# Finer release of attention work in a 512-column mixer, with the first softmax scaling moved into the norm

## The chip, the cores and the metric

The kernel runs on 1 core of a Trainium2 chip. The metric is the device time of one launch in microseconds (us). Before the change it is 2238.53 us, the median of 3 runs (2237.58 to 2239.18).

## The reference

Two layers act on 256 latent tokens and 256 context tokens of 1024 channels. Each layer is a half-weight SwiGLU feed-forward, a mixer, and a second feed-forward, each between RMS norms with modulation. The mixer makes one combined input projection of the normed tokens and runs two branches on it: retention with 4 heads, and differential attention with 8 heads, which the change touches. Context tokens read context tokens only, latent tokens read all 512; the last layer needs the latent output alone.

```python
def diff_attend(q, k, v, lam):
    s = jnp.einsum('bhiqd,bhikd->bhiqk', q, k).astype(jnp.float32) * (DIFF_DH ** -0.5)
    p = jax.nn.softmax(s, axis=-1)
    a = p[:, :, 0] - lam * p[:, :, 1]
    return jnp.einsum('bhqk,bhke->bhqe', a.astype(v.dtype), v)

def diff_output(o, subln_w, lam_init):
    o = rmsnorm(jnp.transpose(o, (0, 2, 1, 3)), subln_w) * (1.0 - lam_init)
    return o.reshape(o.shape[0], o.shape[1], -1)
```

The norm is taken over the 128 channels of one head and one token. EPS is 1e-6.

## The kernel before

Every product in fp32 is three matmuls on TensorE (`mm3`, L340 to L342): the operands are split into a high part and a remainder, and high by high, high by low and low by high are summed in PSUM. Weights are split as they arrive: ScalarE casts (L164), VectorE subtracts (L165). A projection block of the mixer is either `tok` (128 tokens by 512 columns, 24 matmuls) or `projT` (two times 128 channels, 48 matmuls of 512 columns when both token kinds are wanted, of 256 when only latent tokens are). These blocks run one behind the other and are meant to keep TensorE fed. The results of a Q or K block of the attention are turned by the rotary tables on VectorE and split by casts on ScalarE (L567, L571, L572) and subtractions on VectorE (L569).

The attention itself is side work. A generator `diff_attn` handles one pair of heads: `score` issues 4 matmuls into PSUM (L651, L652), takes a row maximum (L653), the exponentials of both maps on ScalarE with their row sums (L659), scales the first map by its reciprocal sum (L665) and adds the second, times minus lambda and its own reciprocal (L666). Three scores later `weigh` transposes the result (L678), copies it out of PSUM (L680) and multiplies it by V (L684). At the fourth `weigh` of a token kind comes the norm tail: square (L689), sum (L691), `rstd_of` on GpSimd (L264 and the power L266), and four scaled writes (L697). In layer 0 a pair of heads has 11 steps (latent and context queries), in layer 1 it has 7. There are four pairs, d0 to d3 below, and four retention heads, r0 to r3, driven in the same way.

`defer` puts a generator into the queue `sideq` with a due time, counted in ticks; `tick` advances the clock at places among the projections and takes steps from the first generator in the queue. `need` runs the queue until a named generator is finished. A tile scheduler then orders the instructions of each engine by what they depend on, so the order on an engine is near the program's but not equal to it. PSUM has 8 banks: a score of latent queries holds 2, a score of context queries 1, a K block 2, the others 1.

```python
n = -(-sideq[0][2] // max(1, sideq[0][1] - clock[0]))
while n > 0 and sideq:
    step()
    n -= 1
```

Of the kernel before, what the change touches and what calls it, by code (L numbers as in the profile page):

```python
# [14 lines left out]
AF = mybir.ActivationFunctionType  # L15
# [5 lines left out]
KD = 8  # L21
# [13 lines left out]
def build(ctx, tc, a):  # L35
# [74 lines left out]
    def slot(shape, dt=F32):  # L110
        return slots.get(shape, dt)
# [7 lines left out]
    def small(n, tag):  # L119
        return sm.tile([P, n], F32, tag=tag, name=tag)  # L120
# [141 lines left out]
    def rstd_of(ss, n, w=1):  # L262
        m = small(8, "rm")
        pool.tensor_scalar(out=m[:, :w], in0=ss, scalar1=1.0 / n, scalar2=EPS, op0=ALU.mult, op1=ALU.add)  # L264
        r = small(8, "rr")
        pool.tensor_tensor(out=r[:, :w], in0=m[:, :w], in1=cneg[:, :w], op=ALU.pow)  # L266
        return r
# [184 lines left out]
    def mixer(l, st, AB, fetch, after):  # L452
# [10 lines left out]
        sideq = deque()  # L463
        done = set()
        pend = []
        clock = [0]

        def step():
            it = sideq[0]
# [7 lines left out]
        def tick():  # L477
            clock[0] += 1
            if sideq:
                n = -(-sideq[0][2] // max(1, sideq[0][1] - clock[0]))  # L480
                while n > 0 and sideq:
                    step()
                    n -= 1

        def defer(key, gen, within, steps):
            sideq.append([gen, clock[0] + within, steps + 1, key])
# [5 lines left out]
        def flush():  # L492
            while pend:
                pend.pop(0)()

        def tok(ws, t, ev):
            bk = bank()
            for k in range(KD):
                wt = ws[k // 2].rearrange("p s (k n) -> p s k n", k=2)
                mm3(bk, h[k // 2][:, k % 2, 0, t * P:(t + 1) * P], h[k // 2][:, k % 2, 1, t * P:(t + 1) * P],  # L500
                    wt[:, 0, k % 2], wt[:, 1, k % 2], k == 0, k == KD - 1)
            flush()
            post = ev(t, bk)
            banks.put(bk)
            if post is not None:
                pend.append(post)
            tick()
# [10 lines left out]
        def projT(b, pairs, ev):  # L518
            ws = [split(r) for r in load(a["winT"][l, b])]
            n = 256 * len(pairs)  # L520
            if len(pairs) == 2:
                b0 = banks.two()
                bk = b0
            else:
                b0 = bank()
                bk = b0.rearrange("p (j n) -> p j n", j=2)
            for j in range(2):
                js = slice(j * P, (j + 1) * P)
                for k in range(KD):
                    wt = ws[k // 4].rearrange("p s (k n) -> p s k n", k=4)  # L530
                    mm3(bk[:, j], wt[:, 0, k % 4, js], wt[:, 1, k % 4, js], h[k // 2][:, k % 2, 0, 0:n],
                        h[k // 2][:, k % 2, 1, 0:n], k == 0, k == KD - 1)
                if j == 0:
                    flush()
                    if len(pairs) == 2:
                        tick()
            for c in pairs:
                ev(c, bk[:, :, c * 256:(c + 1) * 256])
            banks.put(b0)
            tick()  # L540
# [96 lines left out]
        def diff_attn(u, KH, KL, Q, dv):  # L637
            lag = deque()
            ch = (u % 2) * 256

            def score(c, k0, NK, t, hh):
                if c == LAT:
                    b0 = banks.two()
                    sb = b0
                else:
                    b0 = bank()
                    sb = b0.rearrange("p (m n) -> p m n", m=2)
                mx = small(2, "mx")
                for m in range(2):
                    qs = Q[m][:, hh, t * P:(t + 1) * P]  # L650
                    mm(sb[:, m], lhsT=qs, rhs=KH[m][:, hh, k0:k0 + NK], start=True, stop=False)  # L651
                    mm(sb[:, m], lhsT=qs, rhs=KL[m][:, hh, k0:k0 + NK], start=False, stop=True)  # L652
                dve.reduce_max(mx, sb, axis=AX.X)  # L653
                nb = small(2, "nb")
                dve.tensor_scalar(out=nb, in0=mx, scalar1=-0.125, scalar2=None, op0=ALU.mult)
                e = tmp4([P, 2, 512])
                se = small(2, "se")
                for m in range(2):
                    act(e[:, m, :NK], sb[:, m], AF.Exp, bias=nb[:, m:m + 1], scale=0.125, accum_out=se[:, m:m + 1])  # L659
                banks.put(b0)  # L660
                rc = small(2, "rc")
                dve.reciprocal(rc, se)
                r1 = small(1, "r1")
                dve.tensor_tensor(out=r1, in0=rc[:, 1:2], in1=K["nlam"], op=ALU.mult)
                dve.tensor_scalar(out=e[:, 0, :NK], in0=e[:, 0, :NK], scalar1=rc[:, 0:1], scalar2=None, op0=ALU.mult)  # L665
                dve.scalar_tensor_tensor(out=e[:, 0, :NK], in0=e[:, 1, :NK], scalar=r1, in1=e[:, 0, :NK],  # L666
                                         op0=ALU.mult, op1=ALU.add)
                return e[:, 0]

            obs = {}  # L670

            def weigh(c, k0, NK, tt, hh, e):
                if tt == 0 and hh == 0:
                    obs[c] = bank()
                ob = obs[c].rearrange("p (t n) -> p t n", t=2)
                tb = bank()
                for i in range(NK // P):
                    nc.tensor.transpose(tb[:, i * P:(i + 1) * P], e[:, i * P:(i + 1) * P], ident)  # L678
                aT = tmp2()
                nc.scalar.copy(aT[:, :NK], tb[:, :NK])  # L680
                banks.put(tb)
                for i in range(NK // P):
                    kt = k0 // P + i
                    mm(ob[:, tt, hh * P:(hh + 1) * P], lhsT=aT[:, i * P:(i + 1) * P],  # L684
                       rhs=dv[kt // 2][:, kt % 2, ch + hh * P:ch + (hh + 1) * P], start=i == 0, stop=i == NK // P - 1)
                if tt == 0 or hh == 0:
                    return
                sq = tmp2([P, 2, 256])
                act(sq, ob, AF.Square)  # L689
                ss = small(4, "oss")  # L690
                dve.reduce_sum(ss, sq.rearrange("p t (h d) -> p (t h) d", h=2), axis=AX.X)  # L691
                r = rstd_of(ss, P, 4)
                if (u // 2, c) not in o:
                    o[u // 2, c] = slot([P, 2, 512])
                for tt in range(2):
                    for hh in range(2):
                        dve.scalar_tensor_tensor(out=o[u // 2, c][:, tt, ch + hh * P:ch + (hh + 1) * P],  # L697
                                                 in0=ob[:, tt, hh * P:(hh + 1) * P],
                                                 scalar=r[:, 2 * tt + hh:2 * tt + hh + 1], in1=K["sub"],
                                                 op0=ALU.mult, op1=ALU.mult)  # L700
                banks.put(obs[c])

            for c in QP:
                k0, NK = (0, 512) if c == LAT else (256, 256)
                for tt in range(2):
                    for hh in range(2):
                        if len(lag) == LAG:
                            weigh(*lag.popleft())
                        lag.append((c, k0, NK, tt, hh, score(c, k0, NK, 2 * c + tt, hh)))
                        yield  # L710
            while lag:
                weigh(*lag.popleft())
                yield
            slots.put(*KH, *KL, *Q)
            if u % 2:
                slots.put(*dv)
# [140 lines left out]

        rkq = {}

        def rkq_blocks(z):  # L860
            kk = [slot([P, 2, 512], F32R) for _ in range(2)]
            projT(2 + z, BOTH, ev_ret(kk[0], kk[1], 128 ** -0.5))
            qq = [slot([P, 2, 512], F32R) for _ in range(2)]
            projT(z, QP, ev_ret(qq[0], qq[1], 1.0))
            rkq[z] = (kk, qq)
# [9 lines left out]
        def pick(both, lat):  # L875
            return lat if last else both
# [7 lines left out]
            tok(ws, t, ev_V(dv))  # L884
        K.update(mixer_consts())
        kq = diff_blocks(0)
        diff_defer(0, kq, dv, pick(5, 4))
        kq = diff_blocks(1)
        diff_defer(1, kq, dv, pick(6, 5))
        need("d0")  # L890
        rkq_blocks(0)
        rv_block(0, pick(4, 2), pick(8, 5))
        need("d1")
        wide(8, QP, ev_gB(0))
        kq = diff_blocks(2)
# [1 line left out]
        dv = [slot([P, 2, 512]) for _ in range(2)]  # L897
        wide(5, BOTH, ev_V(dv))
        flush()
        diff_defer(2, kq, dv, pick(6, 4))  # L900
        wide(2, QP, ev_rg(0, False))
        kq = diff_blocks(3, "d2")
        diff_defer(3, kq, dv, pick(7, 5))
        wide(6, QP, ev_gA(0))
        rkq_blocks(1)
        need("d3")
        rv_block(1, pick(4, 2), pick(7, 4))
        wide(9, QP, ev_gB(1))
        wide(3, QP, ev_rg(1, True))
        need("r3")  # L910
# [175 lines left out]
```

## Time and profile before

| | |
|---|---|
| median of 3 runs | 2238.53 us |
| the profiled execution, its own time | 2237.81 us |
| its span, first to last instruction | 2236.0 us |
| TensorE busy, share of the span | 96% |
| VectorE, ScalarE, GpSimd busy | 62%, 39%, 6% |
| mean granted TensorE clock, of full speed | 0.986 |

The profile comes from one execution on the chip. "Busy" counts an instruction from its start to its modelled end; in the timeline and in the groups by line the text behind "<-" names the engine, tile and line that ended the idle time before an instruction. In rows of matmuls the issue distance is read from the starts, since one begins while the one before it still drains. A granted clock of 1.0 is TensorE's upper level, 2.4 GHz, and 0.5 is 1.2 GHz.

### The profile page before, as it was taken

Reading aid. Unit: us, or ns where it says so; the run is one execution under the profiler, and the core shown is the slowest. Engines: PE = TensorE matmul, PEld = TensorE weight load, DVE = VectorE, ACT = ScalarE, POOL = GpSimd, SP = SyncE. Lnnn points to the kernel's source line nnn. Section 1 sums busy time; section 2 is a strip of 40 time slices with the busy share of each in tenths; the row PEclk is TensorE's granted clock in tenths of the full one; section 3 lists DMA queues with packets and bytes.
Section 4 is the critical chain, followed back from the end, with each engine's and each line's share of the span. In section 5 each row is a group of like instructions: output and inputs, shape, how many; then the busy total and the mean of one; then the engine's idle time right before and its main releaser. Section 6 shows DMA issues by size and latency. Waiting matters only on the chain. (4 is left out here: it accounts for less than half of the span.)

```text
span 2236.0 us, 27616 instructions
## 1 busy us (share of the span) xinstructions
PE 2150.1 (96%) x10694; PEld 1799.5 (80%) x10694; DVE 1377.9 (62%) x2180; ACT 866.1 (39%) x1367; POOL 131.6 (6%) x248
## 2 busy tenths in 40 slices
PE   7999999989999999999999999999998999898998
PEld 4888888767877888888888788888876788787997
DVE  3798372677667764596243389635257676677454
ACT  3322232564345433532232242223245455455443
POOL 1000000200100010200000110000020010001000
PEclk8999999999999999999999999999999999999999
DMA  9766342211222234465334256724322133355554
GB/s 336 247 224 225 101 135 94 88 47 61 91 69 76 81 102 151 130 206 174 102 110 146 85 174 214 252 95 142 101 71 95 61 112 114 117 179 184 183 187 132
DMA packets 85059, 306.98 MB, mean 137 GB/s; under 512 B 9968, under 2 KB 10048, under 8 KB 84928
## 3 DMA queue, kind: packets, MB, share of 16 engines
q1 hardware_dynamic: 81648, 295.73, 39.9%
q0 software_dynamic: 2848, 8.43, 1.4%
q8 instruction: 83, 1.36, 0.2%
q10 hardware_dynamic: 432, 1.06, 0.1%
q14 instruction: 48, 0.39, 0.1%
HBM read 304.10 MB, written 1.09 MB: 136 GB/s over the span
## 5 line engine op out<-in xcount | busy, mean ns | idle before, releaser
L165 DVE TENSOR_TENSOR w<-raw,w 128x1024 fp32r<-128x1024 f32 x408 | 497.6, 1222 | 442.5 <-ACT w L164 438.6
L164 ACT CAST w<-raw 128x1024 fp32r<-128x1024 f32 x408 | 427.8, 1053 | 645.6 <-PE ps L342 585.4
L340 PE MATMUL ps<-h,w 128*128 128x512 f32 (+1 forms) x1856 | 664.5, 360 | 8.4 <-ACT t L659 7.4
L341 PE MATMUL ps<-h,w 128*128 128x512 f32 (+1 forms) x1856 | 664.2, 358 | 0.0
L342 PE MATMUL ps<-h,w 128*128 128x512 f32 (+1 forms) x1856 | 662.3, 358 | 0.4 <-DVE w L165 0.4
L340 PEld LDWEIGHTS ps<-h,w 128*128 128x128 f32 x1856 | 352.4, 191 | 63.3 <-ACT t L659 8.3
L341 PEld LDWEIGHTS ps<-h,w 128*128 128x128 f32 x1856 | 353.1, 190 | 50.1 <-issue 0.8
L342 PEld LDWEIGHTS ps<-h,w 128*128 128x128 f32 x1856 | 352.2, 190 | 50.3 <-DVE w L165 0.8
L184 DVE CUSTOM_DVE_ANT_0 jd<-r,r 128x1024 bf16<-128x1024 f32 x224 | 273.3, 1220 | 6.4 <-DMA r<-wada_dram 1.6
L340 PE MATMUL ps<-w,h 128*128 128x512 f32 x544 | 212.6, 392 | 3.7 <-ACT t L659 3.1
L341 PE MATMUL ps<-w,h 128*128 128x512 f32 x544 | 212.8, 392 | 0.6 <-DVE w L165 0.6
L342 PE MATMUL ps<-w,h 128*128 128x512 f32 x544 | 212.3, 391 | 0.0
L340 PE MATMUL ps<-w,gs 128*128 128x512 f32 x504 | 196.2, 389 | 0.0
L341 PE MATMUL ps<-w,gs 128*128 128x512 f32 x504 | 196.1, 389 | 0.0
L342 PE MATMUL ps<-w,gs 128*128 128x512 f32 x504 | 196.1, 389 | 0.0
L369 ACT ACTIVATE t<-ps 128x512 f32<-128x512 f32 (+1 forms) x88 | 47.9, 544 | 252.7 <-PE ps L342 252.7
L340 PEld LDWEIGHTS ps<-w,h 128*128 128x128 f32 x544 | 102.2, 188 | 25.1 <-ACT t L659 4.0
L370 DVE TENSOR_TENSOR r<-ps,t 128x512 f32<-128x512 f32 (+1 forms) x88 | 54.7, 622 | 109.4 <-PE ps L342 80.4
L341 PEld LDWEIGHTS ps<-w,h 128*128 128x128 f32 x544 | 102.2, 188 | 21.7 <-DVE w L165 2.2
L342 PEld LDWEIGHTS ps<-w,h 128*128 128x128 f32 x544 | 102.2, 188 | 20.6
L340 PEld LDWEIGHTS ps<-w,gs 128*128 128x128 f32 x504 | 94.6, 188 | 19.8
L342 PEld LDWEIGHTS ps<-w,gs 128*128 128x128 f32 x504 | 94.6, 188 | 19.7
(175 smaller groups left out, 2167.5 us busy)
## 6 DMA issues: line engine op xcount, KB each, us to landing
raw<-fin_dram SPq DMA_DIRECT2D x176, 512.0 KB, 4.2
r<-wada_dram SPq DMA_DIRECT2D x144, 512.0 KB, 5.1
raw<-fout_dram SPq DMA_DIRECT2D x88, 512.0 KB, 3.6
raw<-winW_dram SPq DMA_DIRECT2D x80, 512.0 KB, 3.6
raw<-winT_dram SPq DMA_DIRECT2D x48, 512.0 KB, 4.0
raw<-wout_dram SPq DMA_DIRECT2D x16, 512.0 KB, 5.1
r<-scr POOLq DMA_DIRECT2D x10, 512.0 KB, 5.2
r<-cc_dram SPq DMA_DIRECT2D x7, 512.0 KB, 5.7
```

Of the source, the lines that this page charges most:

```text
L164: keep(nc.scalar.copy(w[:, 0, :], src))
L165: keep(dve.tensor_tensor(out=w[:, 1, :], in0=src, in1=w[:, 0, :], op=ALU.subtract))
L184: dve.tensor_tensor_reduce(out=junk, in0=r[j], in1=cs[c], scale=1.0, scalar=0.0, op0=ALU.mult, op1=ALU.add, accum_out=out[:, c, 2 * u + j: ...
L340: mm(o, lhsT=wH, rhs=xH, start=start, stop=False)
L341: mm(o, lhsT=wH, rhs=xL, start=False, stop=False)
L342: mm(o, lhsT=wL, rhs=xH, start=False, stop=stop)
L369: act(sg[:, :N], ab[0][:, :N], AF.Silu)
L370: dve.tensor_tensor(out=g[f // 2][:, f % 2, :N], in0=ab[1][:, :N], in1=sg[:, :N], op=ALU.mult)
```

## The change

1. The tick now adds steps left over ticks left to a credit and takes a step for each whole unit of it; before, the quotient was rounded up, so at least one step was taken at every tick. Ticks come every 12 matmuls of 512 columns: two in a `tok` block (before: one), four in a `projT` block of both token kinds (before: two), and two in one of latent tokens alone (before: one). The due times are longer in ticks, mostly about twice.
2. d0 has to be finished between the K and the Q block of the first retention projections instead of before them.
3. The first map is no longer divided by its row sum. Its exponentials are used as they are, the second map gets minus lambda times the first sum over the second, and the missing factor is put into the norm: the sum of squares is multiplied by the squared reciprocal of the first sum ahead of the root, and the root's result by the reciprocal. The VectorE operation L665 (48 times) goes away; for each norm tail (12 times) one small VectorE reciprocal and three small GpSimd products come in, two of which stand between the sum and the norm's writes.

```diff
         def tick():
             clock[0] += 1
             if sideq:
-                n = -(-sideq[0][2] // max(1, sideq[0][1] - clock[0]))
-                while n > 0 and sideq:
+                credit[0] += sideq[0][2] / max(1, sideq[0][1] - clock[0])
+                while credit[0] >= 1 and sideq:
                     step()
-                    n -= 1
+                    credit[0] -= 1
+            else:
+                credit[0] = 0
...
                     wt[:, 0, k % 2], wt[:, 1, k % 2], k == 0, k == KD - 1)
+                if k == 3:
+                    tick()
             flush()
...
-                if j == 0:
-                    flush()
-                    if len(pairs) == 2:
+                    if k == 7 and j == 0:
+                        flush()
+                    if j * KD + k in ((3, 7, 11) if len(pairs) == 2 else (7,)):
                         tick()
...
+                if c not in sall:
+                    sall[c] = small(8, "sall").rearrange("p (m i) -> p m i", m=2)
+                i4 = 2 * (t % 2) + hh
...
                 for m in range(2):
-                    act(e[:, m, :NK], sb[:, m], AF.Exp, bias=nb[:, m:m + 1], scale=0.125, accum_out=se[:, m:m + 1])
+                    act(e[:, m, :NK], sb[:, m], AF.Exp, bias=nb[:, m:m + 1], scale=0.125,
+                        accum_out=sall[c][:, m, i4:i4 + 1])
                 banks.put(b0)
-                rc = small(2, "rc")
-                dve.reciprocal(rc, se)
+                rc = small(1, "rc")
+                dve.reciprocal(rc, sall[c][:, 1, i4:i4 + 1])
                 r1 = small(1, "r1")
-                dve.tensor_tensor(out=r1, in0=rc[:, 1:2], in1=K["nlam"], op=ALU.mult)
-                dve.tensor_scalar(out=e[:, 0, :NK], in0=e[:, 0, :NK], scalar1=rc[:, 0:1], scalar2=None, op0=ALU.mult)
+                dve.scalar_tensor_tensor(out=r1, in0=rc, scalar=K["nlam"], in1=sall[c][:, 0, i4:i4 + 1],
+                                         op0=ALU.mult, op1=ALU.mult)
...
                 dve.reduce_sum(ss, sq.rearrange("p t (h d) -> p (t h) d", h=2), axis=AX.X)
+                n0 = small(4, "n0")
+                dve.reciprocal(n0, sall[c][:, 0, :])
+                n2 = small(4, "n2")
+                pool.tensor_tensor(out=n2, in0=n0, in1=n0, op=ALU.mult)
+                pool.tensor_tensor(out=ss, in0=ss, in1=n2, op=ALU.mult)
                 r = rstd_of(ss, P, 4)
+                pool.tensor_tensor(out=r[:, :4], in0=r[:, :4], in1=n0, op=ALU.mult)
...
-        def rkq_blocks(z):
+        def rkq_blocks(z, before=None):
             kk = [slot([P, 2, 512], F32R) for _ in range(2)]
             projT(2 + z, BOTH, ev_ret(kk[0], kk[1], 128 ** -0.5))
+            if before:
+                need(before)
...
-        diff_defer(0, kq, dv, pick(5, 4))
+        diff_defer(0, kq, dv, pick(12, 10))
         kq = diff_blocks(1)
-        diff_defer(1, kq, dv, pick(6, 5))
-        need("d0")
-        rkq_blocks(0)
-        rv_block(0, pick(4, 2), pick(8, 5))
+        diff_defer(1, kq, dv, pick(16, 14))
+        rkq_blocks(0, "d0")
+        rv_block(0, pick(8, 4), pick(16, 10))
...
-        diff_defer(2, kq, dv, pick(6, 4))
+        diff_defer(2, kq, dv, pick(12, 8))
...
-        diff_defer(3, kq, dv, pick(7, 5))
+        diff_defer(3, kq, dv, pick(16, 10))
...
-            rv_block(1, pick(4, 2), pick(7, 4))
+            rv_block(1, pick(8, 4), pick(16, 8))
```

The first number of a pair is for layer 0, the second for layer 1.

How the order of the instructions moves is shown at three places. In these rows an operand named `h` is the mixer's input, `w` a split weight, and what follows "waits" is the engine on whose progress the instruction waits.

The first place is TensorE in layer 1, from the third score of d0 on (the first two stand ahead of these rows in both orders). Before:

```order
L651 MATMUL ps<-r_12378,r_12464 128x512 [waits Activation_49]
L652 MATMUL ps<-r_12380,r_12464 128x512
L651 MATMUL ps<-r_12379,r_12465 128x512 [waits Activation_49]
L652 MATMUL ps<-r_12381,r_12465 128x512
L678 MATMUL ps<-ident,t_12582 128x128 [waits DVE_49]
L678 MATMUL ps<-ident,t_12582 128x128 x3
L651 MATMUL ps<-r_12378,r_12464 128x512 [waits Activation_49]
L652 MATMUL ps<-r_12380,r_12464 128x512
L684 MATMUL ps<-r_12148,t_12614 128x128 [waits Activation_49]
```

And of the change (the scores are L658 and L659 there, the transposes L685, the product with V L691):

```order
L658 MATMUL ps<-r_12370,r_12456 128x512 [waits Activation_49]
L659 MATMUL ps<-r_12372,r_12456 128x512
L658 MATMUL ps<-r_12371,r_12457 128x512 [waits Activation_49]
L659 MATMUL ps<-r_12373,r_12457 128x512
L340 MATMUL ps<-h,w 128x256 [waits Activation_49]
L341 MATMUL ps<-h,w 128x256
L342 MATMUL ps<-h,w 128x256
L340 MATMUL ps<-h,w 128x256
```

Before, the transposes of the first score and the fourth score follow the third score at once, and the 48 projection matmuls of 256 columns of d1's Q block stand in one piece behind d0's third product with V. Now 19 of these 48 stand between the third score and the first transposes, 6 between those and the product with V, and 23 behind the second transposes, ahead of the fourth score.

The second place is ScalarE in the same stretch. Before, the row of L659 for the third score's second map, the copies and the casts of d1's K block up to the fourth score's exponentials:

```order
L659 ACTIVATE t_12628,se<-ps,nb 128x512
L680 COPY t_12690<-ps 128x512 [waits PE_49]
L680 COPY t_12718<-ps 128x512 [waits PE_49,Activation_49]
L567 CAST r_12536<-ps 64x2x256 [waits DVE_49]
L567 CAST r_12536<-t_12662 64x2x256 [waits DVE_49]
L571 CAST r_12536<-t_12662 64x2x256
L567 CAST r_12537<-t_12662 64x2x256
...
L567 CAST r_12537<-ps 64x2x256
L659 ACTIVATE t_12704,se<-ps,nb 128x512 [waits Activation_49]
```

Of the change (the casts are L571, L575 and L576, the exponentials L665, the copies L687):

```order
L665 ACTIVATE t_12603,sall<-ps,nb 128x512
L571 CAST r_12528<-ps 64x2x256 [waits DVE_49]
L687 COPY t_12651<-ps 128x512 [waits PE_49,Activation_49]
L571 CAST r_12528<-t_12623 64x2x256 [waits DVE_49]
...
L571 CAST r_12529<-ps 64x2x256
L665 ACTIVATE t_12665,sall<-ps,nb 128x512 [waits DVE_49]
L575 CAST r_12529<-ps 64x2x256 [waits DVE_49]
...
L687 COPY t_12713<-ps 128x512 [waits PE_49]
...
L665 ACTIVATE t_12727,sall<-ps,nb 128x512 [waits DVE_49,PE_49,Activation_49]
```

Before, the exponentials of three scores stand ahead of the casts and the fourth behind them; now those of two stand ahead and the third behind. Ten casts lie between in both.

The third place is GpSimd at two norm tails of layer 0. Before:

```order
L264 TENSOR_SCALAR rm<-oss 128x4 [waits DVE_49]
L266 TENSOR_TENSOR rr<-rm,cneg 128x4 [waits Pool_49]
L264 TENSOR_SCALAR rm<-oss 128x4 [waits DVE_49]
L266 TENSOR_TENSOR rr<-rm,cneg 128x4 [waits Pool_49]
L784 TENSOR_SCALAR gm<-bmv 128x1 [waits DVE_49]
L785 TENSOR_TENSOR gr<-gm,cneg 128x1 [waits Pool_49]
```

Of the change:

```order
L702 TENSOR_TENSOR n_3516<-n_3514 128x4 [waits DVE_49]
L703 TENSOR_TENSOR oss<-oss,n_3516 128x4 [waits DVE_49,Pool_49]
L264 TENSOR_SCALAR rm<-oss 128x4 [waits Pool_49]
L266 TENSOR_TENSOR rr<-rm,cneg 128x4 [waits Pool_49]
L705 TENSOR_TENSOR rr<-rr,n_3514 128x4 [waits Pool_49]
L702 TENSOR_TENSOR n_3683<-n_3681 128x4 [waits DVE_49]
```

A tail has five rows instead of two; L703 and L705 stand between the sum and the norm's writes.

## Rows read from the trace of the kernel before

**Rows 1.** The page, busy time by engine.

```profile
PE 2150.1 (96%) x10694; PEld 1799.5 (80%) x10694; DVE 1377.9 (62%) x2180; ACT 866.1 (39%) x1367; POOL 131.6 (6%) x248
```

**Rows 2.** Windows: from:to, length, busy (count) by engine, clock, DMA share, GB/s.

```profile
454.00:545.00 91.00, 78.19 (x399) 62.54 (x397) 75.28 (x154) 50.35 (x113) 4.09 (x6) 0.96 0.17 53
640.00:700.00 60.00, 57.88 (x294) 47.52 (x294) 41.16 (x85) 27.91 (x59) 2.43 (x4) 1.00 0.25 80
700.00:760.00 60.00, 54.55 (x280) 45.04 (x279) 45.33 (x88) 33.55 (x72) 1.98 (x4) 0.97 0.19 62
1700.00:1775.00 75.00, 59.54 (x323) 49.03 (x322) 58.45 (x100) 42.04 (x78) 1.59 (x2) 0.89 0.19 62
1850.00:1890.00 40.00, 38.44 (x200) 31.87 (x199) 26.87 (x46) 20.51 (x35) 1.23 (x2) 1.00 0.35 107
1890.00:1940.00 50.00, 42.43 (x222) 35.43 (x221) 37.70 (x63) 27.02 (x47) 1.84 (x3) 0.93 0.37 121
sum 756.00, PE 709.60 PEld 590.20 DVE 528.62 ACT 354.50 POOL 49.55; mean PE 70.96 PEld 59.02 DVE 52.86 ACT 35.45 POOL 4.96
```

**Rows 3.** PE's waits: engine, line, for what: us, times, longest.

```profile
PE ps L651 <- DVE r L569: 11.4, 6, 5.2
PE ps L340 <- ACT t L659: 10.5, 5, 6.4
PE ps L678 <- DVE t L666: 8.5, 6, 3.1
PE ps L651 <- ACT t L659: 8.1, 2, 6.1
```

**Rows 4.** Timeline of ACT and PE around long waits: start, length, instruction, [idle before].

```profile
1732.85 0.58 ACT L567 CAST r<-ps 64x512 fp32r<-64x512 f32 x1
1733.46 0.69 ACT L659 ACTIVATE t<-ps,nb 128x512 f32<-128x512 f32 x1
1734.29 0.79 PE L340 MATMUL ps<-h,w 128*128 128x512 f32 x1 [6.37 <-ACT t L659]
1719.67 1.11 PE L678 MATMUL ps<-ident,t 128*128 128x128 f32 x4 [1.97 <-DVE t L666]
716.39 0.80 PE L651 MATMUL ps<-r,r 128*128 128x512 f32 x1 [5.16 <-DVE r L569]
1916.74 0.66 PE L678 MATMUL ps<-ident,t 128*128 128x128 f32 x4 [3.12 <-DVE t L666]
```

**Rows 5.** Windows of PE alone: length, busy (count), granted clock, DMA.

```profile
722.00:757.00 35.00, 34.71 (x198) 1.00 0.19 60
1734.00:1740.00 6.00, 5.66 (x23) 0.50 0.00 0
1740.00:1746.00 6.00, 6.00 (x45) 1.00 0.08 14
```

**Rows 6.** Timeline of PE, one return from side work to a projection.

```profile
690.33 0.47 PE L342 MATMUL ps<-h,w 128*128 128x512 f32 x1
690.65 0.39 PE L340 MATMUL ps<-h,w 128*128 128x512 f32 x1
690.87 0.39 PE L341 MATMUL ps<-h,w 128*128 128x512 f32 x1
```

**Rows 7.** Groups by line: busy, mean ns | idle before, by what.

```profile
L665 DVE TENSOR_SCALAR t<-t,rc 128x512 f32<-128x512 f32 (+1 forms) x48 | 20.8, 434 | 0.0
L662 DVE RECIPROCAL rc<-se 128x2 f32<-128x2 f32 x48 | 7.6, 159 | 10.3 <-ACT t L659 10.0
L697 DVE SCALAR_TENSOR_TENSOR r<-ps,rr,sub 128x128 f32<-128x128 f32 x48 | 13.7, 344 | 13.8 <-POOL rr L266 13.7
L264 POOL TENSOR_SCALAR rm<-oss 128x4 f32<-128x4 f32 x12 | 3.0, 251 | 428.1 <-DVE oss L691 238.4 <-DVE rc L662 135.7 <-DVE nb L655 54.1
L266 POOL TENSOR_TENSOR rr<-rm,cneg 128x4 f32<-128x4 f32 x12 | 12.4, 1033 | 1.0
```

More of the change, by code (lines that the diff above doesn't have):

```diff
@@ L465, in mixer @@
         pend = []
-        clock = [0]
+        clock, credit = [0], [0]
         def step():
@@ L656, in score @@
                 e = tmp4([P, 2, 512])
-                se = small(2, "se")
                 for m in range(2):
-                    act(e[:, m, :NK], sb[:, m], AF.Exp, bias=nb[:, m:m + 1], scale=0.125, accum_out=se[:, m:m + 1])
+                    act(e[:, m, :NK], sb[:, m], AF.Exp, bias=nb[:, m:m + 1], scale=0.125,
+                        accum_out=sall[c][:, m, i4:i4 + 1])
                 banks.put(b0)
-                rc = small(2, "rc")
-                dve.reciprocal(rc, se)
+                rc = small(1, "rc")
+                dve.reciprocal(rc, sall[c][:, 1, i4:i4 + 1])
                 r1 = small(1, "r1")
-                dve.tensor_tensor(out=r1, in0=rc[:, 1:2], in1=K["nlam"], op=ALU.mult)
-                dve.tensor_scalar(out=e[:, 0, :NK], in0=e[:, 0, :NK], scalar1=rc[:, 0:1], scalar2=None, op0=ALU.mult)
+                dve.scalar_tensor_tensor(out=r1, in0=rc, scalar=K["nlam"], in1=sall[c][:, 0, i4:i4 + 1],
+                                         op0=ALU.mult, op1=ALU.mult)
                 dve.scalar_tensor_tensor(out=e[:, 0, :NK], in0=e[:, 1, :NK], scalar=r1, in1=e[:, 0, :NK],
@@ L668, in score @@
                 return e[:, 0]
-            obs = {}
+            obs, sall = {}, {}
             def weigh(c, k0, NK, tt, hh, e):
```

## The prediction

> **What bounds the kernel now.** I read the page first: TensorE (PE) is busy for 96% of the span [rows 1]. So only three things are left to win: its idle time, time at the half clock, and matmuls. The change removes no matmul. The windows over the two mixers come next [rows 2]: of 756.0 us PE is busy 709.6, so 46.4 us are idle, and nearly all of that lies in six stretches. These are d0 and d1 of layer 0 (454:545, 12.8 idle), d2 (640:700, 2.1) and d3 (700:760, 5.5) of layer 0; d0 and d1 of layer 1 (1700:1775, 15.5), d2 (1850:1890, 1.6) and d3 (1890:1940, 7.6). The clock column shows the second loss. Busy time times the missing part of the clock gives 78.2 x 0.04 = 3.1, 54.6 x 0.03 = 1.6, 59.5 x 0.11 = 6.5 and 42.4 x 0.07 = 3.0: 14.2 us. So the change can take at most about 60 us, 2.7%, away from PE.
>
> The waits of PE [rows 3] say what these idles are: scores waiting for Q's split (L569), or for a bank that an exponential frees (L659), and transposes waiting for the combined maps (L666). The timeline [rows 4] shows the pattern. At 1734.29 PE has stood for 6.37 us: the exponential that frees its bank began at 1733.46, right behind the last of ten casts of d1's K block. The half clock follows such an idle: 1734:1740 runs at 0.50, 1740:1746 at 1.00, while 722:757, side work between projections without a long idle, runs at 1.00 throughout [rows 5]. The idle times come from bunching: side work is issued in a block, and projections that could cover its waits stand behind it.
>
> **The change part by part.** All sums are against the profiled execution, 2237.81 us; the median is 0.7 us above it.
>
> *Layer 1, d0 and d1 (22.0 us of idle and half clock).* The new order puts the 48 Q matmuls of 256 columns between the scores, transposes and sums, 19 + 6 + 23. At the full clock 45 matmuls there take 6.0 us, 0.133 each [rows 5], so 48 give 6.4 us of work to lay under the waits of 6.37 and 1.97 us [rows 4]. With the long idle gone, the half clock behind it goes too: 5.66 x 0.5 = 2.8 us. That is 9.2 us. The rest stays: the ten casts still stand between the exponentials of consecutive scores, now ahead of the third, and the first scores still wait for the splits. Lower bound 3 (the waits only change their place and the half clock goes); upper 15 (6.37, 1.97 and all 6.5 of the clock). I take **9.2**, as the covering work is at hand.
>
> *Layer 0, d3 (7.1).* The first score stands for 5.16 us waiting for L569 at 716.39 [rows 4]. In the new order 23 projection matmuls instead of 10 stand ahead of it. At 0.225 us each (0.22 between the last two starts of [rows 6]) the 13 cover 2.9 us; about 2.2 stay, and with them most of the half clock. **2.9**, between 0 (Q's split comes as much later) and 6.8 (the whole wait and the 1.6).
>
> *Layer 1, d3 (10.6).* In the new order 14 projection matmuls, 3.2 us, stand between the third score and the first transposes, which waited 3.12 us at 1916.74 [rows 4], and the fourth score is moved behind them. But 11 instead of 16 stand ahead of the first scores, which takes 5 x 0.225 = 1.1 us of cover from the Q split. The half clock, 3.0, began at that wait; half of it, 1.5, should go. 3.1 - 1.1 + 1.5 = **3.5**, between 0 and 6.1 (3.12 and all 3.0).
>
> *d2 in both layers (2.1 and 1.6 idle).* Three scores in a row filled the banks and PE waited for the first to come free. Now there are 12 matmuls, 2.7 us, between one score and the next. I take nearly all of it: **3.4**, between 0 and 3.7.
>
> *Layer 0, d0 and d1 (15.9).* For d0 the order stays bunched: all seven scores still come with only 14 projection matmuls among them, and the long wait behind the casts has nothing new beneath it. What shortens the chain is L665, 0.43 us [rows 7], gone from between exponential and transpose: four times, **1.7**, between 0 and 7.8 (with the 6.1 us of the longest such wait [rows 3]).
>
> *L665 elsewhere.* It frees 48 x 0.434 = 20.8 us of VectorE, which is busy 62%; where PE doesn't wait for VectorE this is worth nothing, and where it does, it is counted above.
>
> *Costs.* PE's order has 37 more switches between projection and side work (445 for 408). One return to a projection costs 0.32 - 0.225 = 0.095 us [rows 6]: **-3.5**. At none is 0, at both ends of each 7.
>
> *The norm tail.* L703 and L705 lengthen the chain from the sum to the norm's writes. No row has such a product; L264, the nearest in kind, takes 251 ns, and the power L266, on as many elements, 1033 [rows 7]. So a tail grows by 0.5 to 2.1 us, and I take 0.5, since a product is nearer to L264. VectorE already stands in front of L697 for 13.7 us, 1.15 a tail, and PE's waits name L697 nowhere. I count **0** for PE; the cover is the projection matmuls now between side steps (12, 2.7 us, in most places). If that is gone, the whole 12 x 0.5 = 6 to 25 us is paid, since behind L697 VectorE's queue holds the next reductions and weight splits. The Trainium skill (GPSIMD Engine Reference, "4.1 Engine selection") says that elementwise work on two tensors belongs on VectorE and runs about twice as long on GpSimd; by VectorE's 159 ns for a small reciprocal [rows 7] a product would be about 0.32 us, an estimate, and a tail 0.64 instead of 0.5: the sum stays the same as long as the cover holds. The added reciprocal on VectorE (12 x 0.16) needs no square and lies beside ScalarE's work.
>
> Sum: 9.2 + 2.9 + 3.5 + 3.4 + 1.7 - 3.5 = 17.2. With it the profiled execution would take 2220.6 us, and the median **2221.3**.
>
> **The rivals.**
>
> *The waits move but don't go.* Ten casts, 0.6 us each, still stand in one piece in ScalarE's queue, and what PE does meanwhile needs banks that come free behind them. For it: the order of ScalarE. Against it: a Q block needs one bank and a score two. Then layer 1's d0 gives 3 instead of 9.2, and layer 1's d3 nothing: 17.2 - 6.2 - 3.5 = 7.5, so 2231. Chance 0.21.
>
> *More goes.* If the even spacing ends the half clock in the mixers, and the freed VectorE shortens the splits that the first scores wait for, each term reaches its upper bound but layer 0's d0: 15 + 6.8 + 6.1 + 3.7 + 1.7 - 3.5 = 29.8, so 2209. For it: 722:757. Against it: the first scores of each pair still need the splits. Chance 0.14.
>
> *The norm tail holds VectorE.* Each tail stops VectorE's queue for its two products, and with projections dense on both sides, the splits L165 and the next reductions come late on PE. It decides against the change when a tail costs PE more than (17.2 + 4.5) / 12 = 1.8 us; at the upper price, 2.1, the time is 2238.5 - 17.2 + 25 = 2246. For it: VectorE waits for the power at nearly every tail. Against it: VectorE has 38% of the span free, and PE has not waited there. Chance 0.07.
>
> *The clock oscillates.* More, shorter gaps of PE could drop the clock again and again: two more stretches at the half clock like 1734:1740 in each of the six would cost 12 x 2.8 = 34 us, and the time is 2255. Against it: 722:757 has side work in small pieces at 1.00 [rows 5]. The Trainium skill (TensorE: Matmul & The Clock Gate, "A second HAM failure mode: psum-queue depth-cycling") describes a kernel whose clock swings because PE idles briefly and often between groups of matmuls; this trace disagrees so far, with the 1.00 of that stretch. Chance 0.03.
>
> *It doesn't do what it says.* The scheduler orders by dependences, and at layer 0's d0 it has undone the spreading. If execution shifts the waits likewise in the other stretches, the tail's first 6 us and the switches eat what L665 gives: within 4 us of before. Chance 0.07.
>
> **How the numbers follow.** The forecast, at 0.48, is 2221.3 us, with its own range 2214 to 2227. A difference of 0.2%, 4.5 us, is about what a measurement of this kernel can tell from no change. Faster by more: 0.48 + 0.14 + 0.20 of the 0.21 = 0.82. Within it: 0.07 + 0.01 + 0.01 of the tail's case = 0.09. Slower: 0.06 + 0.03 = 0.09. The range 2207 to 2234 takes in the first rival and most of the second, and leaves out the slow cases and no change.
>
> **What would show it.** Right: in the waits of PE on an exponential and on the combined maps (L651, L340 and L678 before), the 6.37 us at layer 1's d0 is gone or under 2, and that stretch's granted clock is over 0.95; layer 0's d3 still has a wait of 1.5 to 3 us for the Q split; layer 0's d0 keeps one of about 6 us behind the casts. VectorE's busy time falls by about 20 us with no gain for PE in the feed-forwards. Wrong: a wait of over 4 us in layer 1's d0 in another place, half clock in stretches now at 1.00, or waits of PE for the norm's writes or for weight splits behind them.

## The result, and the profile after

The changed kernel takes 2224.35 us (median of 4 runs, 2223.84 to 2227.77), against 2238.06 for the kernel before in the same runs: a ratio of 0.9942, 95% interval 0.9924 to 0.9959. The forecast was 2221.3 with a range of 2207 to 2234. So the direction and the range held, and 13.7 us were won where 17.2 were expected.

The page of the changed kernel, busy time by engine (its span is 2222.3 us):

```profile
PE 2149.8 (97%) x10694; PEld 1795.9 (81%) x10694; DVE 1367.4 (62%) x2144; ACT 866.1 (39%) x1367; POOL 140.3 (6%) x284
```

PE's busy time is what it was [rows 1], and VectorE's fell by 10.5 us; what went is PE's idle time. The windows show from where; the columns are those of [rows 2], and layer 1 now lies some 3 to 18 us earlier, so its windows only roughly hold the same work:

```profile
454.00:545.00 91.00, 78.53 (x392) 62.68 (x391) 70.90 (x133) 48.53 (x104) 3.81 (x11) 0.96 0.18 58
700.00:760.00 60.00, 57.64 (x293) 47.24 (x291) 45.00 (x85) 34.00 (x71) 1.99 (x6) 0.97 0.23 71
1700.00:1775.00 75.00, 68.93 (x383) 56.29 (x382) 57.38 (x97) 42.47 (x80) 3.85 (x10) 1.00 0.23 71
1890.00:1940.00 50.00, 47.54 (x249) 39.53 (x249) 35.45 (x60) 24.16 (x42) 3.40 (x7) 0.96 0.40 130
```

At 1700:1775 PE is idle for 6.1 us where it was 15.5, and the granted clock there is 1.00 for 0.89. At 454:545 nothing has changed. The retention stretches of layer 1 have become worse; here is that of r2 and r3 (windows of PE alone, from:to and then the columns of [rows 5]):

```profile
1950.00:2000.00 50.00, 47.90 (x240) 0.97 0.58 191
1970.00:1980.00 10.00, 8.28 (x44) 0.83 0.27 80
```

The same work ran without a gap at 1.00 in the kernel before, where it lay some 14 us later:

```profile
1965.00:2015.00 50.00, 50.00 (x256) 1.00 0.65 215
```

PE's waits (engine, line, for what: us, times, longest) give the new list, to be held against [rows 3]:

```profile
PE ps L340 <- ACT r L575: 9.3, 2, 6.8
PE ps L340 <- DVE t L772: 5.3, 4, 2.2
PE ps L658 <- DVE r L573: 4.8, 3, 2.4
PE ps L658 <- ACT t L665: 4.5, 2, 2.5
PE ps L685 <- DVE t L673: 3.6, 5, 1.2
```

L573, L575, L658, L665, L673 and L685 are the former L569, L571, L651, L659, L666 and L678. The second line is new in size: L772, the former L759, is a product of a retention head, and before PE waited for it for 0.8 us in all and 0.4 at most.

Windows don't say what a stretch is worth once the work has shifted. A count does: both traces hold 7200 projection matmuls of the feed-forwards and mixers (L340 to L342 with `h` and `w`) in nearly the same sequence, so the start of the n-th can be compared. This table gives, for single profiled runs, by how much each stretch became longer or shorter against the kernel before (in brackets, the time at which the stretch ends in the kernel before, at the start of the next such matmul). The labels are those of the experiments below.

| stretch | forecast | the change | e12 | e6 | e3 | e11 | e9 |
|---|---|---|---|---|---|---|---|
| up to n = 1800 (639.4): layer 0, d0, d1, r0, r1 | -1.7 | +0.5 | +5.6 | +3.2 | -0.3 | -0.6 | +0.2 |
| to 2640 (929.9): layer 0, d2, d3, r2, r3 | -4.8 | -3.6 | -3.8 | +2.5 | -4.2 | -0.4 | -5.4 |
| to 5100 (1702.1): feed-forwards | 0 | +0.3 | +1.7 | +1.7 | +0.1 | 0.0 | 0.0 |
| to 5400 (1802.0): layer 1, d0, d1 | -9.2 | -13.5 | -10.6 | -8.5 | -11.5 | -9.0 | -9.9 |
| to 5580 (1846.9): r0, r1 | 0 | +3.2 | +3.1 | -4.4 | +0.9 | -0.2 | +1.7 |
| to 5760 (1893.9): d2 | -1.5 | -1.9 | -1.9 | -1.9 | -1.9 | 0.0 | +0.6 |
| to 5940 (1951.7): d3 | -3.5 | -2.6 | -2.6 | -2.6 | -4.2 | -0.4 | -9.4 |
| to 6240 (2054.1): r2, r3 | 0 | +3.9 | +4.2 | -0.9 | +0.8 | 0.0 | +0.8 |
| switches, all stretches | +3.5 | in the above | | | | | |
| sum | -17.2 | -13.7 | -4.3 | -11.0 | -20.3 | -10.6 | -21.4 |

A side step that falls on the other side of a mark shifts a few us between neighbouring rows (e6 at r0, r1 is such a case). The feed-forwards, which no edit touches, differ by up to 1.7 us; a difference of that size says nothing. The forecast's places were right; missing in it are the 3.2 and 3.9 us that the retention heads of layer 1 lost. The timeline shows three waits of the changed kernel that the experiments turn on (start, length, instruction, idle before):

```profile
485.69 0.79 PE L340 MATMUL ps<-h,w 128*128 128x512 f32 x1 [6.84 <-ACT r L575]
1803.69 0.39 PE L340 MATMUL ps<-r,r 128*128 128x256 f32 x1 [2.25 <-DVE t L772]
1971.72 0.39 PE L340 MATMUL ps<-r,r 128*128 128x256 f32 x1 [2.10 <-DVE t L772]
```

The first is layer 0's d0, the others are the second heads of a pair (r1 and r3) in layer 1. Behind r1's wait the chain reads, on ScalarE and VectorE:

```profile
1800.61 0.71 ACT L750 ACTIVATE W<-t,lg,lg 128x384 f32<-128x384 f32 x1 [3.77 <-DMA t<-strip_dram]
1800.61 0.42 DVE L743 TENSOR_SCALAR t<-t,lg 128x384 f32<-128x384 f32 x1 [2.17 <-DMA t<-strip_dram]
1803.21 0.76 DVE L772 TENSOR_TENSOR t<-ps,W 128x256 f32<-128x256 f32 x2
```

A head's first step fetches the table of positions for its decay weights; both engines wait for that transfer, three small operations on ScalarE and six on VectorE follow, and only 2.6 us after it lands comes the product that PE needs. How much work covers the transfer depends on when GpSimd issues it. Two rows each, from the kernel before and from the changed one (L784 and the former L785, now L798, belong to the norm of r0, the head ahead of r1):

```profile
1808.93 0.55 POOL L727 DMA_DIRECT2D t<-strip_dram  x1 [28.62 <-DVE W L734]
1818.00 0.23 POOL L784 TENSOR_SCALAR gm<-bmv 128x1 f32<-128x1 f32 x1 [8.52 <-DVE bmv L782]
1795.35 1.40 POOL L798 TENSOR_TENSOR gr<-gm,cneg 128x1 f32<-128x1 f32 x1
1796.70 0.64 POOL L740 DMA_DIRECT2D t<-strip_dram  x1
```

Before, the fetch stood 9 us ahead of that norm, and PE had 8.3 us of work from its issue to the matmul that needs the product (1817.21). Now it stands right behind the norm, and PE has 4.7 us (to 1801.44, where the wait begins). For r3 it is the same.

### The profile page after: what moved, and what is told of

Read it like the earlier page. It is cut to its first block, busy times and chain, and to the rows that moved or that the text cites. A ratio compares the mean times of both kernels' runs of the same rounds, so it can differ in the third digit from the quotient of the medians.

```text
span 2222.3 us, 27632 instructions
## 1 busy us (share of the span) xinstructions
PE 2149.8 (97%) x10694; PEld 1795.9 (81%) x10694; DVE 1367.4 (62%) x2144; ACT 866.1 (39%) x1367; POOL 140.3 (6%) x284
## 5 line engine op out<-in xcount | busy, mean ns | idle before, releaser
L340 PE MATMUL ps<-h,w 128*128 128x512 f32 (+1 forms) x1856 | 665.3, 360 | 9.8 <-ACT r L575 6.8
L342 PE MATMUL ps<-h,w 128*128 128x512 f32 (+1 forms) x1856 | 663.2, 358 | 0.7 <-DVE w L165 0.7
L340 PEld LDWEIGHTS ps<-h,w 128*128 128x128 f32 x1856 | 351.0, 190 | 64.7 <-ACT r L575 7.0
L342 PEld LDWEIGHTS ps<-h,w 128*128 128x128 f32 x1856 | 351.0, 189 | 51.2 <-DVE w L165 1.1
L340 PE MATMUL ps<-w,h 128*128 128x512 f32 x544 | 214.9, 396 | 3.2 <-ACT r L575 2.5
L342 PE MATMUL ps<-w,h 128*128 128x512 f32 x544 | 213.1, 392 | 0.0
L340 PE MATMUL ps<-w,gs 128*128 128x512 f32 x504 | 196.2, 389 | 0.0
L342 PE MATMUL ps<-w,gs 128*128 128x512 f32 x504 | 196.1, 389 | 0.0
L340 PEld LDWEIGHTS ps<-w,h 128*128 128x128 f32 x544 | 103.0, 189 | 24.5 <-ACT r L575 2.9
L342 PEld LDWEIGHTS ps<-w,h 128*128 128x128 f32 x544 | 102.8, 189 | 20.8
L340 PEld LDWEIGHTS ps<-w,gs 128*128 128x128 f32 x504 | 94.6, 188 | 19.9
L342 PEld LDWEIGHTS ps<-w,gs 128*128 128x128 f32 x504 | 94.6, 188 | 19.6
```

The lines of the kernel that those rows point to most:

```text
L340: mm(o, lhsT=wH, rhs=xH, start=start, stop=False)
L342: mm(o, lhsT=wL, rhs=xH, start=False, stop=stop)
```

## The experiments

The theory to begin with: the even spacing of the steps made the gain, the folding little, and the finer ticks uncovered the retention heads. The rivals: the folding made the gain; or the longer norm tail took part of it away.

**e1, the folding alone.** Of the change only this part:

```diff
-                dve.tensor_scalar(out=e[:, 0, :NK], in0=e[:, 0, :NK], scalar1=rc[:, 0:1], scalar2=None, op0=ALU.mult)
...
+                pool.tensor_tensor(out=n2, in0=n0, in1=n0, op=ALU.mult)
+                pool.tensor_tensor(out=ss, in0=ss, in1=n2, op=ALU.mult)
```

> The kernel before with the folding alone; ticks, due times and the place where d0 is needed are as before. The theory that the spacing of the side work made the gain expects 0 to 3 us less than before (about 2236.5), with the 6.4 us wait in layer 1's first pair still there. The rival, that the 20.8 us taken from VectorE made the gain, expects 8 us or more less (2230 or lower). If the two added products on GpSimd hold VectorE, it is slower than before by 6 us or more.

2237.54 us, ratio 0.9998 (0.9989 to 1.0008): nothing. The long wait of layer 1's d0 is still there, at 5.1 us instead of 6.4 (first line, the same wait as the second of [rows 3]); that of layer 0's d0 is 4.3 for 6.1 (second line). The third is the page:

```profile
PE ps L340 <- ACT t L661: 8.3, 3, 5.1
PE ps L654 <- ACT t L661: 6.7, 3, 4.3
PE 2156.4 (96%) x10694; PEld 1802.1 (81%) x10694; DVE 1366.4 (61%) x2144; ACT 865.9 (39%) x1367; POOL 138.8 (6%) x284
```

VectorE's busy time falls by 11.5 us, and PE's idle time in this one profile by 6.4. But PE's busy time is 6.3 us longer, in part at a lower clock (0.94 for 0.97 at 700:760), so the time stays. The rival that the folding made the gain falls.

**e2, the change without the folding.**

> The change without the folding: credit, ticks every 12 matmuls, new due times, d0 needed later. The theory that the spacing made the gain expects 2224 to 2228. The rival that the folding made it expects 2234 or more. If the longer norm tail costs, this one is faster than the changed kernel, 2222 or less.

2222.66 us, ratio 0.9933 (0.9918 to 0.9948), against 0.9942 (0.9924 to 0.9959) with the folding. The gain is all here. Whether the tail costs something like 0.1% can't be read from these two intervals.

**e3, the position table kept.** The table is fetched once per layer instead of by each head:

```diff
-            strip = tmp2([P, 384])
-            pool.dma_start(strip, a["strip"])
+            strip = K["strip"]
```

> The changed kernel, with the position table of the retention decay fetched once per layer ahead of the attention and kept, where each of the four retention heads fetches it anew in its first step. Theory: the waits of 2.25 and 2.10 us on L772 in layer 1, new in the changed kernel, come from that fetch and the six operations behind it, which 12 matmuls no longer cover; then both fall under 0.5 us, the half clock behind them goes, and the time is 2224.35 - 4 to 5, about 2220. Rival: the single buffer of the decay weights W, free only when the head before is through, holds them; then the waits stay within 0.5 us of what they are and the time within 1 us.

2218.44 us, ratio 0.9917 (0.9902 to 0.9931). The table above has +0.9 and +0.8 for the two retention stretches instead of +3.2 and +3.9. That the fetch was part of the chain is shown. The waits themselves only fell to 1.50 and 1.14 us, not under 0.5:

```profile
PE ps L340 <- DVE t L773: 2.6, 2, 1.5
```

What is left is not the single buffer of W, which the rival named: for r1 ScalarE writes to it from 1789.96 on, well ahead of the wait. It is a second transfer of the same step, the head's norm weights, for which VectorE stands right ahead of its last two operations on W (for r3 by 1.20 us):

```profile
1789.96 0.71 ACT L751 ACTIVATE W<-strip,lg,lg 128x384 f32<-128x384 f32 x1
1801.57 0.29 DVE L738 TENSOR_SCALAR gnb<-gnb 128x256 f32<-128x256 f32 x1 [1.57 <-DMA gnb<-gnw_dram]
```

No run takes this second transfer away.

**e4, the context half out of PSUM first.**

```diff
-            for c in pairs:
+            for c in reversed(pairs):
                 ev(c, bk[:, :, c * 256:(c + 1) * 256])
```

> The changed kernel, with the context half of a projection block taken out of PSUM before the latent half. Theory: the 6.84 us for which PE waits on a cast of L575 in layer 0's first pair is the bank of d1's K block, which is not free before its last cast out of PSUM; with these casts first the wait falls to 2 to 4 us and the time by 3 to 6 us with the half clock behind it, to about 2219 to 2221. Rival: the casts of the latent half, then last, hold the exponentials and PE instead, and the wait stays at 6 to 7 us; then 2223 to 2226.

2222.31 us, ratio 0.9929 (0.9913 to 0.9946). At layer 0's d0 PE gets 4.3 us more work done in the same 91 us, and no wait there is as long as 6.84 us:

```profile
454.00:545.00 91.00, 82.84 (x415) 66.35 (x414) 72.89 (x141) 49.34 (x108) 5.44 (x15) 0.96 0.19 57
```

So that wait was the bank behind the late casts. But elsewhere other waits grew, those of scores on an exponential to 10.4 us in all (5 times), and 2 us are left of the gain, inside the uncertainty.

**e5, e3 and e4 together.**

> The changed kernel with both edits of before: the decay's position table kept, and the context half of a projection block taken out of PSUM first. If their savings lie on different waits they add: 5.9 and 2.0 us off 2224.35, about 2216.5. If the shorter wait in layer 0 only moves work onto the waits of the other stretches (the table-free waits and the half clock vary from kernel to kernel), 2217.5 to 2220.

2215.41 us, ratio 0.9893 (0.9878 to 0.9907), 1.07% below the kernel before: as far as the intervals tell, they add.

**e6, the quotient rounded up again, the finer ticks kept.**

```diff
-                credit[0] += sideq[0][2] / max(1, sideq[0][1] - clock[0])
-                while credit[0] >= 1 and sideq:
+                n = -(-sideq[0][2] // max(1, sideq[0][1] - clock[0]))
+                while n > 0 and sideq:
```

> The changed kernel with the quotient rounded up again at each tick, everything else of the change kept. Theory: the finer ticks make the gain and the credit little; then 2222 to 2228. Rival: without the credit at least one step falls on every tick, the side work bunches as before and most of the gain goes, 2230 to 2237.

2226.71 us, ratio 0.9942 (0.9927 to 0.9957), as fast as the change with the credit. With ticks every 12 matmuls the credit isn't needed for the total, though the table shows another sum: layer 0 loses 5.6 us, and the retention heads of layer 1 lose nothing. There the fetching step and the product's step of r1 lie 12 matmuls apart as in the change, and PE doesn't wait: r0 runs a tick earlier, the fetch goes out at 1804.36, and PE has 8.0 us of work before it needs the product. So it isn't the distance of 12 matmuls that uncovers the fetch.

**e7, the credit and the folding, without the finer ticks.**

> The kernel before with the folding and the credit, but ticks, due times and the place where d0 is needed as before (one tick per 24 matmuls). Theory: several steps still fall on one tick, so the waits stay: 2234 to 2239, like the folding alone. Rival: the credit makes the gain: 2222 to 2228.

2220.05 us, ratio 0.9914 (0.9898 to 0.9931). My theory falls: the credit at the old ticks gives the whole gain, and rather more. Either of the two parts alone breaks what had cost the time, and the finer ticks have a price of their own on top.

**e8, e3 without the folding.**

> The changed kernel with the position table kept and the folding undone. The folding alone gave nothing. If it gives nothing here either, 2217 to 2220, the same as with the folding (2218.4). If the longer norm tail costs where side work is spread, it is faster than that by 1.5 us or more; if the freed VectorE is of use there, it is slower by 1.5 us or more.

2216.51 us, ratio 0.9898 (0.9884 to 0.9913), against 0.9917 (0.9902 to 0.9931) with the folding. The median is 1.9 us lower, but the intervals overlap. Together with e1 and e2: the folding brings nothing in any surrounding, and its cost, if it has one, is some 0.1 to 0.2% and not clear of the noise. In the single traces it would lie in layer 1's d3, which gains 6.3 us in e2 and 6.0 in e8, and 2.6 in the change and 4.2 in e3.

**e9, the credit alone.** The kernel before with the first hunk of the change and nothing else.

> The kernel before with the credit alone: no folding, no finer ticks, the old due times and places. In layer 1 d0 then takes 2, 3 and 3 steps at its three ticks instead of 3, 3 and 2. Theory after the last runs: that is enough, and the folding plays no part: 2219 to 2223, a ratio of 0.990 to 0.993. Rival: the folding was needed beside the credit (it takes 0.43 us from each chain that PE waits for): 2227 or more.

2216.55 us, ratio 0.9907 (0.9892 to 0.9923): 21 us below the kernel before. The windows of layer 1's d0 and d3:

```profile
1700.00:1775.00 75.00, 67.58 (x367) 56.44 (x366) 58.98 (x104) 39.45 (x74) 4.00 (x5) 0.93 0.22 66
1890.00:1940.00 50.00, 50.00 (x269) 42.01 (x268) 36.01 (x61) 23.65 (x41) 2.80 (x4) 1.00 0.43 131
```

In the second, PE is busy without a gap, where it was idle for 7.6 us. Counted from the code, d0 of layer 1 takes 2, 2 and 3 steps at its three ticks instead of 3, 2 and 2, and d3 takes 1, 2, 2 and 2 instead of 2, 2, 2 and 1 (the last step of a pair is empty; the expectations of e9 and e11 count one step too many). PE's wait for a retention product is at most 0.5 us here; the fetch for r1 goes out ahead of r0's norm, as in the kernel before.

**e10, the credit alone with the edits of e3 and e4.**

> The credit alone, with the position table kept and the context half taken out of PSUM first. With ticks every 24 matmuls the retention heads don't wait for the table, so that edit should give nothing here; the other should give up to 4 us at layer 0's d0. If so 2216 to 2220. If the order it brings puts the first scores of layer 1 together again (12 score matmuls, then 8 transposes and 8 products, stand in one piece there in the order), the wait of 4 to 7 us is back and the time is 2224 to 2230.

2214.66 us, ratio 0.9898 (0.9884 to 0.9911). The feared order did not bring the wait back, but the two edits add nothing that can be told from e9's 0.9907.

**e11, one number.** What does the credit do to layer 1's d0? It has 7 steps left and at its first tick 3 ticks left; the quotient 7/3 is rounded up to 3, with the credit 2 are taken. Two are also taken with a due time one tick later (7/4):

```diff
-        diff_defer(0, kq, dv, pick(5, 4))
+        diff_defer(0, kq, dv, pick(5, 5))
```

> The kernel before with one number changed: in layer 1 d0 is due after 5 ticks, not 4, so it takes 2 steps at each of three ticks instead of 3, 3, 2. If the third step at the first tick causes the 6.4 us wait, that wait falls under 2 us with the half clock behind it, and the time falls by 7 to 10 us to 2228 to 2231, while d3 of layer 1 keeps its waits of 7.6 us in all. Rival: the gain there needs the finer spacing; then within 3 us of before.

2229.43 us, ratio 0.9962 (0.995 to 0.9975): 8.2 us from one number. PE's wait for a bank of that stretch, 10.5 us in all and 6.4 at most before [rows 3], is now

```profile
PE ps L340 <- ACT t L659: 4.3, 5, 1.6
```

and in the windows the stretch of d0 and d1 has 66.69 us of work where there were 59.54, while d3's stays as it was:

```profile
1700.00:1775.00 75.00, 66.69 (x363) 55.63 (x362) 61.86 (x109) 42.89 (x80) 4.00 (x5) 0.93 0.25 76
1890.00:1940.00 50.00, 43.13 (x221) 35.74 (x220) 37.62 (x62) 24.05 (x42) 2.47 (x4) 0.90 0.40 128
```

In PE's order the fourth score now stands behind 32 of the 48 Q matmuls, at 1729.20, where it stood ahead of all of them. Behind the casts on ScalarE there is now the exponential of the third score, at 1728.46, where it was that of the fourth, at 1733.46 [rows 4]; while the casts run, PE has the Q block to work on.

**e12, d0 needed early again, in the changed kernel.**

> The changed kernel with d0 needed before the K block of the retention projections, as before the change. At that place four steps of d0 are still open in both layers and would run in one piece. If that bunch costs a wait, 2226 to 2232; if the projections on both sides cover it, 2222 to 2226.

2231.29 us, ratio 0.9969 (0.9956 to 0.9981): 7 us of the change's 13.7 are lost, most of it in the stretches of d0, whose last steps `need` then runs at once (three by the count from the code, the last of them empty): 5.0 us in layer 0 and 2.9 in layer 1, by the table. In layer 1 a score waits for a cast as long as this:

```profile
1732.22 0.80 PE L658 MATMUL ps<-r,r 128*128 128x512 f32 x1 [3.25 <-ACT r L575]
```

## Why the prediction was right, and where not

**The bound.** Right: what went is idle time of the bunched stretches, PE's busy time didn't move, and the largest gain lies where it was put. That the sum came within 3.5 us is in part luck: 4.3 us too little in layer 1's d0 and d1 stand against 7.1 us of losses that it left out.

**Layer 1, d0 and d1: 9.2 forecast, 13.5 measured (12.3 without the folding, by the same count on e2).** The mechanism was right: the 6.37 us wait is gone, the longest wait of that stretch is 2.00, and the granted clock of the whole stretch is 1.00. The size was off mostly by the clock: I counted 2.8 us of the 6.5 as won, and all of it went. Right, too, that the casts stay and that the first scores still wait.

**But not for the reason in the change's name.** I put the gain down to the spacing by 12 matmuls. e9 and e11 show that the spacing isn't needed. One step too many at the first tick puts the fourth score ahead of the Q block, and its exponential behind ten casts; any edit that takes it away (credit, finer ticks, a later due time) brings 8.5 to 13.5 us in this stretch.

**Layer 0, d3 and d2: 4.8 forecast, 3.6 measured.** The wait for Q's split at 716 fell from 5.16 to 2.36 us; 2.2 were forecast. **Layer 1, d2 and d3: 5.0 forecast, 4.5 measured.** The 3.12 us wait is gone, and new ones of 2.48 and 2.46 stand in the stretch.

**Layer 0, d0: 1.7 forecast, +0.5 measured.** The step "what shortens the chain is L665" failed. e1 takes L665 away at the old ticks, and its longest wait there falls from 6.1 to 4.3 us, but the stretch gains only 0.4 us. In the changed kernel the long wait is 6.84 us: as forecast, it stayed. What ends it there is the last cast out of PSUM (L575), as e4 shows, and no shorter chain of maps reaches that.

**The norm tail: 0 forecast.** The products take 224 (L703) and 199 ns (L705); 251 was taken from the nearest row. VectorE waits longer in front of the norm's writes, 21.3 us instead of 13.7 [rows 7], 0.63 us a tail, and PE names L710 nowhere:

```profile
L710 DVE SCALAR_TENSOR_TENSOR r<-ps,rr,sub 128x128 f32<-128x128 f32 x48 | 13.5, 345 | 21.3 <-POOL rr L705 21.3
L703 POOL TENSOR_TENSOR oss<-oss,n 128x4 f32<-128x4 f32 x12 | 2.7, 224 | 97.4 <-DVE oss L698 79.0 <-DVE nb L662 18.4
L705 POOL TENSOR_TENSOR rr<-rr,n 128x4 f32<-128x4 f32 x12 | 2.4, 199 | 0.9
```

The cover held, and that rival falls by e1 and e8. VectorE's busy time fell by 10.5 us where about 20 were named as a sign. The estimate of 0.32 us that the prediction worked out from the Trainium skill (GPSIMD Engine Reference, "4.1 Engine selection") is above the 0.22 us that these rows show.

**The clock.** The rival of a swinging clock falls: with many small switches the six stretches of the attention are at 0.96 to 1.00, and it is a wait of a retention head, not the switches, that has the half clock behind it at 1970:1980. What the Trainium skill (TensorE: Matmul & The Clock Gate, "A second HAM failure mode: psum-queue depth-cycling") describes, a clock that swings because PE idles briefly and often, doesn't show at this spacing. One sign of being wrong did come true: stretches that were at 1.00 now have some half clock, 1850:1890 with 0.96 and 1950:2000 with 0.97. The 3.5 us for the switches can't be told apart: PE's busy time stayed although the clock gave time back at 1700:1775, so about as much was added elsewhere, and no run says by what.

**The term that was missing.** The retention heads, +3.2 and +3.9 us. The change also moved their ticks, and I priced none of the 8 retention generators. It isn't that 12 matmuls between two steps cover less than 24: before, the fetching step of r1 and of r3 fell on the same tick as the step with the product (4 steps over 3 ticks or 2, 2 at once), and e6 has the 12 without the loss. What was lost is the early issue of the fetch, ahead of the first head's norm on GpSimd. The rows that would have shown it were in the trace: the table's transfer and the decay operations behind it. e3, without the transfer, gives most of it back. That its place on GpSimd decides is read from the traces; no run moves the fetch alone. With the two losses priced the sum would have come to 10 us, and with d0's clock in full to 14.

**What stays open.** In e9 d3 of layer 1 gains 9.4 us, and that of layer 0 is idle for 1.8 us where it was for 5.5. As in layer 1's d0, the credit takes one step fewer at the first tick, 1 for 2 in both layers (7/4 and 11/6, rounded up before), and on PE the first two scores, one row of eight matmuls before, stand apart. No run changes d3's due time alone, as e11 does for d0, so this isn't shown. Nor does a step fewer always gain: layer 0's d0 and layer 1's d2 have 2 for 3 in e9, and their stretches change by +0.2 and +0.6.

## What to carry to other kernels

Where side work fills the gaps of one busy engine, look first at how many steps fall on one tick: a single rounding, or one due time, can put a step ahead of a block whose resource it holds, and a change that spreads the work more finely then gets a credit that belongs to the missing step. Take each part of such a change alone before keeping it; here one part of three gave more than all together. And when ticks move, look for every kind of side work that shares them at what its steps prepare for their successors, transfers above all: at which place in the issuing engine's order the transfer stands, and how much work lies between its issue and its use.

## What was not expected of the hardware

An idle of PE of 2 us can be followed by the half clock, and a later one of the same length not: in the changed kernel the window 1700:1775 has 1.00 with waits of 2.00 and 1.97 us in it, while 1970:1980, with r3's wait of 2.10 us, has 0.83. A sum of waits alone therefore doesn't give the time: in e1 PE's idle time fell by 6.4 us and its time not at all.
